# Latent-attention value products in unsplit float32, 64 columns wide, two query tiles in the two halves of TensorE's columns

## The chip, the cores and the metric

The kernel runs on one core of a Trainium2 chip. The metric is the device time of the whole program in microseconds (us). TensorE (PE) does matrix products into PSUM, VectorE (DVE), ScalarE (ACT) and GpSimd (POOL) do the elementwise work, and SyncE (SP) issues most transfers. "PEld" in a profile is PE's loading of the stationary operand.

## The reference

Two layers of an encoder with three kinds of attention side by side. The change is in the first kind, latent attention with 6 heads over 1,024 positions:

```python
kv = (rms_norm(c_kv, kv_lat_g) @ w_ukv).reshape(B, S, 6, 64 + 64)
k_nope, v_mla = kv[..., :64], kv[..., 64:]
...
s = jnp.einsum('bqhd,bkhd->bhqk', qi, k) * 96 ** -0.5     # qi: 128 queries
p = jax.nn.softmax(s, axis=-1)
o = jnp.einsum('bhqk,bkhe->bqhe', p, v)                   # v: 1,024 x 64 per head
```

The result, times a gate `silu(g_mla)`, goes to the output projection with those of the other two kinds.

## The kernel before

Each layer runs in stages: projections with the latent up-projection inside them (`kv_up`), differential attention (DiffItem, lines 720 to 790), neighbourhood attention (`na_item`, lines 1006 to 1048), latent attention (`mla_item`, from line 1161), output projection. Latent attention takes 48 items per layer: 6 heads times 8 query tiles of 128. Beside the items run, per head, the building of queries (`mla_q`) and keys (`mla_kn`, `mla_kt`), and towards the end the loading of the output weights (`load_wo`, casts at line 1229).

An item has three parts. `first`: six matmuls of scores into a PSUM tile S (lines 1172 to 1174; operands split into a high part in TensorE's rounded float32 form, fp32r, and a low remainder), a row maximum on DVE (L1177, L1178), the exponential on ACT (L1180), and normalising on POOL (L1182). `second`: eight PE transposes of the weights into two PSUM tiles T (L650); ACT copies each to the high part in SBUF (L138), then DVE subtracts to get the low part (L653). `third`, once per two query tiles (a pair): 16 matmuls (L1200) into the one PSUM tile O. There the stationary operand holds the value's high part in 64 columns and its low part in the other 64, and high and low weights of both query tiles (256 columns) stream through, so O's two halves are added at the end:

```python
for hl in range(2):
    PE.matmul(box["o"], mla[f"v{e}"][:, k], mla["PT"][b][:, hl, k], start=..., stop=...)
...
copy_act(u[m:m + 64], O[o:o + 64])
V.tensor_tensor(u[m:m + 64], O[m:m + 64], u[m:m + 64], ALU.add)
```

and POOL multiplies the sum into the gate (L1209). `kv_up`, 8 position tiles per layer, makes each head's values in the split form, with ACT for the high and DVE (L550) for the low part, and SP stores them in DRAM (`v_d`), from where POOL's queue fetches one head at a time (L1110).

The order of instructions on each engine is set when the program is built; each engine then runs its own list in order. PE's list is a mixture of the parts of neighbouring items. The tiles O have one buffer, S and T two each.

Of the kernel before, what the change touches and what calls it, by code (L numbers as in the profile page):

```python
# [12 lines left out]
F32 = mybir.dt.float32  # L13
F32R = mybir.dt.float32r
AF = mybir.ActivationFunctionType
ALU = mybir.AluOpType
# [11 lines left out]
    T=2,  # L28
# [14 lines left out]
def hybrid_encoder_kernel(  # L43
# [42 lines left out]
    dp = ctx.enter_context(tc.tile_pool(name="dp", bufs=1, space=bass.MemoryType.DRAM))  # L86
    xmid = dp.tile([S, D], F32, name="xmid")
    nk_d = dp.tile([128, 8, 384], F32, name="nk_d")
    v_d = dp.tile([8, 128, 6, 128], F32, name="v_d")
    wq_d = dp.tile([128, 3072], F32, name="wq_d")  # L90
    rpb_rep = dp.tile([depth * NA_H, 15, 64, 127], F32, name="rpb_rep")

# [44 lines left out]
    def copy_act(o, i, scale=1.0):  # L137
        A.activation(o, i, AF.Copy, scale=scale)  # L138
# [286 lines left out]
    for l in range(depth):  # L425
# [85 lines left out]

        kv_w = T(bp, "n1k", [128, 3072], F32R)
        wkv = kv_w[:, 0:1536].rearrange("p (l a h n) -> p l a h n", l=2, a=2, h=6)
        vst = Ring([kv_w[:, 1536 + i * 768:2304 + i * 768].rearrange("p (j e n) -> p j e n", e=2, n=128) for i in range(2)])
        raw = rawtile([128, 768])
        nc.sync.dma_start(raw, w_ukv[l])
        raw = raw.rearrange("p (h a n) -> p a h n", h=6, a=2)
# [2 lines left out]
            V.tensor_scalar(wkv[:, 0, a], raw[:, a], gcol, None, ALU.mult)  # L522
            V.scalar_tensor_tensor(wkv[:, 1, a], raw[:, a], gcol, f(wkv[:, 0, a]), ALU.mult, ALU.subtract)
        lkv = T(bp, "n1v", [128, 2, 1024], F32R)
        nk_t = T(bp, "n1q", [128, 8, 384])
        st_k = T(cp, "st_k", [128, 8, 6])
        rs_k = T(cp, "rs_k", [128, 8, 6])

# [6 lines left out]
        def kv_up(tt):  # L535
            hi, lo = (lkv[:, i, tt * 128:(tt + 1) * 128] for i in range(2))
            ps = psS()
            for a in range(2):
                o = ps[:, a * 512:a * 512 + 384]
                w0, w1 = (wkv[:, i, a].rearrange("p h n -> p (h n)") for i in range(2))  # L540
                PE.matmul(o, hi, w0, start=True, stop=False)
                PE.matmul(o, hi, w1, start=False, stop=False)
                PE.matmul(o, lo, w0, start=False, stop=True)
            V.tensor_copy(nk_t[:, tt], ps[:, 0:384])
            sumsq(ps[:, 0:384], 384, [(0, 384, 64, st_k[:, tt])], True)
            v = vst()
            pv = ps[:, 512:896].rearrange("p (j e n) -> p j e n", e=2, n=64)
            for e in range(2):
                copy_act(v[:, :, e, e * 64:e * 64 + 64], pv[:, :, e])
                V.tensor_tensor(v[:, :, e, 64 - e * 64:128 - e * 64], pv[:, :, e], f(v[:, :, e, e * 64:e * 64 + 64]), ALU.subtract)  # L550
            nc.sync.dma_start(v_d[tt], f(v).rearrange("p j e n -> p (j e) n"))

        def k_norm():
            V.tensor_tensor(st_k, st_k, st_lat[:, 2].unsqueeze(2).to_broadcast([128, 8, 6]), ALU.add)
            rstd_newton(rs_k.rearrange("p a b -> p (a b)"), st_k.rearrange("p a b -> p (a b)"), 96, 48)
            nc.sync.dma_start(nk_d, nk_t)

        pt = latent_t(2)
        copy_act(lkv[:, 0], pt)
# [511 lines left out]
        def mla_setup():  # L1071

            w = T(bp, "nd", [128, 6144], F32R)
            wq = w[:, 0:3072].rearrange("p (k l h n) -> p k l h n", k=2, l=2, h=6)
            mla["wq"] = wq
            for kc in range(2):
                raw = T(cp, "t2", [128, 640])[:, 0:576]
                nc.sync.dma_start(raw, w_uq[l, kc * 128:(kc + 1) * 128])
                raw = raw.rearrange("p (h n) -> p h n", h=6)
                gcol = vT[l][:, 32 + kc:33 + kc]  # L1080
                hi, lo = wq[:, kc, 0], wq[:, kc, 1]
                for a, b, d in ((0, 96, 0), (80, 96, 96), (64, 80, 112)):
                    n = b - a
                    V.tensor_scalar(hi[:, :, d:d + n], raw[:, :, a:b], gcol, None, ALU.mult)
                    V.scalar_tensor_tensor(lo[:, :, d:d + n], raw[:, :, a:b], gcol, f(hi[:, :, d:d + n]), ALU.mult, ALU.subtract)
            mla["v0"], mla["v1"] = (w[:, 3072 + i * 1024:4096 + i * 1024].rearrange("p (t d) -> p t d", t=8) for i in range(2))
            t = T(bp, "n1q", [128, 3, 1024], F32R)
            mla["lat"] = [t[:, i] for i in range(3)] + [w[:, 5120:6144]]
            mla["free"] = [w[:, i * 1024:(i + 1) * 1024] for i in range(3)] + mla["lat"][3:4] + mla["lat"][0:3]
            mla["free_v"] = [w[:, 3072 + i * 1024:4096 + i * 1024] for i in range(2)]  # L1090
            for kc in range(2):
                hi, lo = mla["lat"][2 * kc:2 * kc + 2]
                (V.tensor_copy if OPT["mla"]["lat"] == "V" else copy_act)(hi, latq[:, kc])
                G.tensor_tensor(lo, latq[:, kc], f(hi), ALU.subtract)
# [66 lines left out]
        def mla_item(h, qt):  # L1161
            e, b = h % 2, (qt // 2) % 2
            qhi, qlo, khi, klo = (forms[:, i] for i in ((0, 1, 6, 7), (2, 3, 4, 5))[e])
            ts_ = slice(qt * 128, (qt + 1) * 128)
            qs = slice(qt % 2 * 128, (qt % 2 + 1) * 128)
            box = {}

            def first():
                ps = psS()
                for a in range(2):  # L1170
                    o, ks = ps[:, a * 512:(a + 1) * 512], slice(a * 512, (a + 1) * 512)
                    PE.matmul(o, qhi[:, ts_], khi[:, ks], start=True, stop=False)  # L1172
# [12 lines left out]
            def second():  # L1185
                if "PT" not in mla:
                    mla["PT"] = {}
                if b not in mla["PT"]:
                    mla["PT"][b] = T(bp, f"R1{b}", [128, 2, 8, 256], F32R)
                PT = mla["PT"][b]  # L1190
                for kh in range(2):
                    ks = slice(kh * 4, kh * 4 + 4)
                    transpose_split(lambda i: box["p"][:, (kh * 4 + i) * 128:(kh * 4 + i + 1) * 128],
                                    PT[:, 0, ks, qs], PT[:, 1, ks, qs], 4)

            def pv(k):
                if k == 0:
                    box["o"] = psO()[:, 0:256]
                for hl in range(2):
                    PE.matmul(box["o"], mla[f"v{e}"][:, k], mla["PT"][b][:, hl, k], start=(k == 0 and hl == 0), stop=(k == 7 and hl == 1))  # L1200

            def finish():
                O = box["o"]
                u = T(cp, "t2", [128, 640])[:, 0:256]
                m, o = (64, 0) if e else (0, 64)
                copy_act(u[m:m + 64], O[o:o + 64])
                V.tensor_tensor(u[m:m + 64], O[m:m + 64], u[m:m + 64], ALU.add)
                g = sg[m:m + 64, h // 2, (qt // 2) * 256:(qt // 2 + 1) * 256]
# [165 lines left out]
```

## Time and profile before

| what | us |
|---|---|
| runs of the kernel before: median (lowest to highest of 3) | 1851.77 (1850.18 to 1853.68) |
| the profiled execution's own time | 1856.72 |
| its span, first to last instruction | 1854.9 |
| PE busy in the span | 1720.4 (93%) |
| DVE busy | 1338.3 (72%) |
| ACT busy | 947.9 (51%) |
| POOL busy | 811.2 (44%) |

Busy time is the union of an engine's instructions. A PE instruction counts until its last result is written, while the next is already streaming, so what a matmul takes of PE in a row of matmuls is read from start to start, not from its duration. The mean granted TensorE clock is 0.979 of full speed. A row of windows further down has these columns: the stretch, its length, busy time and instructions of PE, PEld, DVE, ACT and POOL, the granted clock, the share of the DMA engines and GB/s.

### The profile page before, as it was taken

What the parts mean: (1) busy time and instruction counts of PE and PEld (TensorE: products, weight loads), DVE (VectorE), ACT (ScalarE), POOL (GpSimd) and SP (SyncE); (2) the same over time, 40 slices, a digit from 0 to 9 for tenths busy, and PEclk for the clock granted to TensorE, in tenths of its full rate; (3) what the DMA queues carried; (4) which work ended last, traced back from release to release, by engine and by line L of the source; (5) the groups of instructions that cost most, each with busy time, mean ns of one, the idle gap of its engine ahead of it and who ended that gap; (6) DMA issues with size and microseconds to landing.
All of it is one profiled execution on the core that took longest, in us unless ns stands there. A gap on an engine that the chain in (4) does not pass through costs nothing. (4 is left out here: it accounts for less than half of the span.)

```text
span 1854.9 us, 28846 instructions
## 1 busy us (share of the span) xinstructions
PE 1720.4 (93%) x10724; PEld 1471.2 (79%) x10724; DVE 1338.3 (72%) x2634; ACT 947.9 (51%) x1954; POOL 811.2 (44%) x756
## 2 busy tenths in 40 slices
PE   4998889989899999989998988899999999999998
PEld 3978667778798888978878877777889888898877
DVE  6879877765975679995576487778565656999742
ACT  6522577771057667753342227777512765776500
POOL 4422435533345545473225043555415564556532
PEclk9999899999999999999999989999999999999999
DMA  9356000104323101131232520001221140003022
GB/s 285 100 131 168 13 24 23 35 1 123 104 55 54 59 1 24 35 89 33 80 127 59 109 82 23 24 12 35 66 86 29 21 102 1 12 24 81 23 91 91
DMA packets 141036, 117.60 MB, mean 63 GB/s; under 512 B 39834, under 2 KB 126048, under 8 KB 140384
## 3 DMA queue, kind: packets, MB, share of 16 engines
q1 hardware_dynamic: 116716, 103.61, 19.1%
q0 software_dynamic: 12480, 6.29, 2.0%
q10 hardware_dynamic: 11700, 5.85, 1.7%
q8 instruction: 85, 1.39, 0.3%
q14 instruction: 55, 0.45, 0.1%
HBM read 97.91 MB, written 23.68 MB: 66 GB/s over the span
## 5 line engine op out<-in xcount | busy, mean ns | idle before, releaser
L138 ACT ACTIVATE R<-T 128x512 fp32r<-128x512 f32 (+1 forms) x336 | 180.8, 550 | 125.5 <-PE T L638 61.8
L620 PE MATMUL F<-R,Pb 128*128 128x512 f32 x766 | 233.8, 420 | 11.7 <-ACT sg L138 11.7
L620 PEld LDWEIGHTS F<-R,Pb 128*128 128x128 f32 x766 | 141.5, 197 | 48.3 <-ACT sg L138 18.6
L1182 POOL TENSOR_SCALAR Pb<-Pb,sm 128x1024 f32<-128x1024 f32 x96 | 110.4, 1151 | 138.3 <-DVE sm L1178 69.3
L731 DVE TENSOR_REDUCE sm<-S 128x1 f32<-128x1024 f32 x128 | 153.2, 1218 | 16.0 <-PE S L726 14.5
L653 DVE TENSOR_TENSOR R<-T,R 128x512 fp32r<-128x512 f32 x192 | 129.1, 681 | 21.0 <-ACT R L138 20.1
L1180 ACT ACTIVATE Pb<-S,sm,rs_q 128x1024 f32<-128x1024 f32 x96 | 115.6, 1204 | 30.1 <-DVE sm L1178 26.4
L1200 PE MATMUL O<-R,nd 128*128 128x256 f32 x768 | 118.3, 292 | 6.3 <-DVE R L653 6.2
L1042 PE MATMUL O<-R,n1v 128*64 128x128 f32 x864 | 120.0, 280 | 1.2 <-ACT R L138 1.2
L1177 DVE TENSOR_REDUCE sm<-S 128x1 f32<-128x1024 f32 x96 | 116.5, 1213 | 5.4 <-PE S L1174 5.2
L650 PE MATMUL T<-ident,Pb 128*128 128x128 f32 x768 | 112.1, 275 | 6.8 <-DVE R L653 6.8
L1024 POOL TENSOR_SCALAR Pb<-Pb,sm 128x512 f32<-128x512 f32 (+1 forms) x96 | 74.5, 780 | 93.2 <-DVE sm L1023 87.7
L1200 PEld LDWEIGHTS O<-R,nd 128*128 128x128 f32 x768 | 102.9, 191 | 13.3 <-DVE R L653 9.1
L1042 PEld LDWEIGHTS O<-R,n1v 128*64 128x64 f32 x864 | 91.1, 136 | 21.7 <-issue 11.1
L1306 POOL TENSOR_TENSOR raw<-sg,raw 128x512 fp32r<-128x512 f32 x32 | 50.0, 1562 | 120.4 <-DVE raw L1305 120.3
L650 PEld LDWEIGHTS T<-ident,Pb 128*128 128x128 f32 x768 | 89.8, 142 | 16.1 <-DVE R L653 5.0
L801 POOL TENSOR_TENSOR Pb<-raw,Pb 128x512 fp32r<-128x512 f32 x32 | 43.8, 1372 | 125.2 <-DVE Pb L800 87.9
L733 ACT ACTIVATE nd<-S,sm 128x1024 f32<-128x1024 f32 x64 | 71.4, 1116 | 47.9 <-DVE sm L731 47.0
L457 ACT ACTIVATE t<-T 128x512 f32<-128x512 f32 x32 | 19.2, 599 | 141.9 <-DVE n1k L933 73.3
L737 POOL TENSOR_SCALAR nd<-nd,sm 128x1024 f32<-128x1024 f32 x48 | 58.7, 1223 | 65.0 <-DVE sm L735 64.8
L733 ACT ACTIVATE sg<-S,sm 128x1024 f32<-128x1024 f32 x64 | 71.3, 1115 | 27.7 <-DVE sm L731 14.1
L1172 PE MATMUL S<-R 128*128 128x512 f32 x192 | 84.8, 443 | 0.3
(439 smaller groups left out, 5247.4 us busy)
## 6 DMA issues: line engine op xcount, KB each, us to landing
raw<-in_w_in_dram SPq DMA_DIRECT2D x32, 512.0 KB
t<-in_ada_w_dram SPq DMA_DIRECT2D x40, 256.0 KB
n1k<-in_w_out_dram SPq DMA_DIRECT2D x16, 512.0 KB
v_d<-n1k SPq DMA_DIRECT2D x16, 384.0 KB
nl<-in_ada_w_dram SPq DMA_DIRECT2D x24, 256.0 KB
nd<-v_d POOLq DMA_DIRECT2D x12, 512.0 KB, 4.9
rpb_rep<-in_na_rpb_dram ACTq DMA_DIRECT2D x12, 476.2 KB
R<-in_ada_w_dram SPq DMA_DIRECT2D x8, 512.0 KB
```

The costliest lines, as they stand in the source:

```text
L138: A.activation(o, i, AF.Copy, scale=scale)
L620: ins = fn()
L650: PE.transpose(pt[:, i * 128:(i + 1) * 128], src_cols(i), ident)
L653: V.tensor_tensor(lo4, pv, f(hi4), ALU.subtract)
L731: V.tensor_reduce(stt[:, m:m + 1], ps, AX.X, ALU.max, negate=True)
L733: A.activation(p, ps.rearrange("p (k n) -> p k n", k=8), AF.Exp, bias=stt[:, m:m + 1], accum_out=stt[:, 2 + m:3 + m])
L1042: PE.matmul(O[m:m + 64, qs], nv[:, c0 + i, h * 64:(h + 1) * 64], PTf[qb][:, i, qs], start=(i == 0), stop=(i == n - 1), skip_group_check=True)
L1172: PE.matmul(o, qhi[:, ts_], khi[:, ks], start=True, stop=False)
L1177: V.tensor_reduce(stt[:, 0:1], ps, AX.X, ALU.max, negate=True)
L1180: A.activation(p, ps, AF.Exp, bias=stt[:, 3:4], scale=rs, accum_out=stt[:, 1:2])
L1182: mla["g"] = G.tensor_scalar(p, p, stt[:, 2:3], 0.0, ALU.mult, ALU.add)
L1200: PE.matmul(box["o"], mla[f"v{e}"][:, k], mla["PT"][b][:, hl, k], start=(k == 0 and hl == 0), stop=(k == 7 and hl == 1))
```

## The change

The values are stored and fetched unsplit, 64 columns per head. The weights are copied from PSUM unsplit, the first T tile of an item by ACT and the second by DVE. Each value product is a float32 matmul with a stationary operand of 64 columns: query tile 0 of the pair into partitions 0 to 63 of O, tile 1 into partitions 64 to 127, alternating. The end is one DVE multiplication per query tile of O with the gate; ACT's copy, DVE's addition and POOL's multiplication are gone.

```diff
-    v_d = dp.tile([8, 128, 6, 128], F32, name="v_d")
+    v_d = dp.tile([8, 128, 6, 64], F32, name="v_d")
...
-            V.tensor_copy(nk_t[:, tt], ps[:, 0:384])
+            kv = kvs()
+            V.tensor_copy(kv[:, 0:384], ps[:, 0:384])
+            copy_act(kv[:, 384:768], ps[:, 512:896])
             sumsq(ps[:, 0:384], 384, [(0, 384, 64, st_k[:, tt])], True)
-            v = vst()
-            pv = ps[:, 512:896].rearrange("p (j e n) -> p j e n", e=2, n=64)
-            for e in range(2):
-                copy_act(v[:, :, e, e * 64:e * 64 + 64], pv[:, :, e])
-                V.tensor_tensor(v[:, :, e, 64 - e * 64:128 - e * 64], pv[:, :, e], f(v[:, :, e, e * 64:e * 64 + 64]), ALU.subtract)
-            nc.sync.dma_start(v_d[tt], f(v).rearrange("p j e n -> p (j e) n"))
+            nc.sync.dma_start(nk_d[:, tt], kv[:, 0:384])
+            nc.sync.dma_start(v_d[tt], kv[:, 384:768].rearrange("p (h n) -> p h n", n=64))
...
-            nc.sync.dma_start(nk_d, nk_t)
...
                 for kh in range(2):
-                    ks = slice(kh * 4, kh * 4 + 4)
-                    transpose_split(lambda i: box["p"][:, (kh * 4 + i) * 128:(kh * 4 + i + 1) * 128],
-                                    PT[:, 0, ks, qs], PT[:, 1, ks, qs], 4)
+                    transpose_plain(lambda i: box["p"][:, (kh * 4 + i) * 128:(kh * 4 + i + 1) * 128],
+                                    mla["PT"][b][:, kh * 4:kh * 4 + 4, qs], 4, kh == 0)
 
             def pv(k):
+
                 if k == 0:
-                    box["o"] = psO()[:, 0:256]
-                for hl in range(2):
-                    PE.matmul(box["o"], mla[f"v{e}"][:, k], mla["PT"][b][:, hl, k], start=(k == 0 and hl == 0), stop=(k == 7 and hl == 1))
+                    box["o"] = psO()[:, 0:128]
+                for t in range(2):
+                    PE.matmul(box["o"][t * 64:t * 64 + 64], mla[f"v{e}"][:, k], mla["PT"][b][:, k, t * 128:(t + 1) * 128],
+                              start=(k == 0), stop=(k == 7), skip_group_check=True)
 
             def finish():
-                O = box["o"]
-                u = T(cp, "t2", [128, 640])[:, 0:256]
-                m, o = (64, 0) if e else (0, 64)
-                copy_act(u[m:m + 64], O[o:o + 64])
-                V.tensor_tensor(u[m:m + 64], O[m:m + 64], u[m:m + 64], ALU.add)
-                g = sg[m:m + 64, h // 2, (qt // 2) * 256:(qt // 2 + 1) * 256]
-                (V if h == MLA_H - 1 and qt == 7 else G).tensor_tensor(g, g, u[m:m + 64], ALU.mult)
+                m = 64 * e
+                for t in range(2):
+                    g = sg[m:m + 64, h // 2, (qt - 1 + t) * 128:(qt + t) * 128]
+                    V.tensor_tensor(g, g, box["o"][t * 64:t * 64 + 64], ALU.mult)
```

PE's list in the middle of a latent stage, before: L1172 to L1174 are scores, L650 transposes of weights, L1156 transposes of a key, L1200 the value products, which stand in two pieces of 9 and 7.

```order
L1174 MATMUL S_14641<-R_1460_12735 128x512
L1200 MATMUL O_14592<-R_1726_14400,nd_14027 128x256 x9
L650 MATMUL T_14627<-ident_75,Pb_12844 128x128 x4
L1156 MATMUL F_14735<-ident_75,n1k_14054 128x128 x4
L1200 MATMUL O_14592<-R_1726_14400,nd_14027 128x256 x7
L650 MATMUL T_14634<-ident_75,Pb_12844 128x128 x4
L1172 MATMUL S_14689<-R_1460_12735 128x512
```

The same place in the changed program (the line numbers are shifted: L634 transposes of weights, L1168 to L1170 scores, L1116 and L1117 a query, L1195 the value products):

```order
L634 MATMUL T_6984<-ident_75,Pb_4657 128x128 x4
L1195 MATMUL O_6996<-R_740_6073,nd_5840 64x128
L634 MATMUL T_6990<-ident_75,Pb_4657 128x128 x4
...
L1170 MATMUL S_7040<-R_489_4520 128x512
L1195 MATMUL O_6996<-R_740_6073,nd_5840 64x128 x8
L634 MATMUL T_7028<-ident_75,Pb_4657 128x128 x4
L1116 MATMUL F_7176<-n1q_5857,nd_5840 128x512
L1117 MATMUL F_7176<-n1q_5857,nd_5840 128x512
L1195 MATMUL O_6996<-R_740_6073,nd_5840 64x128 x7
L634 MATMUL T_7034<-ident_75,Pb_4657 128x128 x4
```

The 16 products of a pair now stand in pieces of 1, 8 and 7, between other matmuls that use all 128 columns. So it is in 42 of the 48 pairs of the program; in the other 6 the pieces are 1 and 15. That makes 138 pieces, where there were 114 before.

DVE's list around the end of a pair, before: L653 is the low part of the weights, L1207 the addition of O's halves, the rest belongs to the softmax and the queries.

```order
L653 TENSOR_TENSOR R_740_6090<-T_7401,R_740_6090 128x4x128
L1207 TENSOR_TENSOR t_911_7384<-O_7367,t_911_7384 64x256
L653 TENSOR_TENSOR R_740_6090<-T_7408,R_740_6090 128x4x128
L1177 TENSOR_REDUCE sm_7470<-S_7463 128x1
L1181 RECIPROCAL sm_7422<-sm_7422 128x1
L1178 TENSOR_TENSOR sm_7470<-sm_7470,rs_q_5886 128x1
```

And in the changed program: L639 is the copy of an item's second T tile, L1202 the multiplication with the gate.

```order
L639 COPY R_740_6073<-T_7331 128x4x128
L1173 TENSOR_REDUCE sm_7388<-S_7381 128x1
L1177 RECIPROCAL sm_7363<-sm_7363 128x1
L1174 TENSOR_TENSOR sm_7388<-sm_7388,rs_q_5869 128x1
L1202 TENSOR_TENSOR sg_1652<-sg_1652,O_7337 64x128 x2
L639 COPY R_758_6207<-T_7375 128x4x128
```

One copy per item stands where two subtractions stood, and the end of a pair is two small multiplications in the place of one addition.

## Rows read from the trace of the kernel before

**Rows 1.** Windows: busy us (instructions) of each engine in stretches of both latent stages.

```profile
668.00:795.00 127.00, 126.47 (x847) 113.38 (x847) 119.31 (x250) 93.09 (x180) 64.17 (x66) 1.00 0.11 26
795.00:850.00 55.00, 47.86 (x305) 41.08 (x303) 52.74 (x89) 34.00 (x63) 36.87 (x29) 0.97 0.23 66
...
1568.00:1697.00 129.00, 127.95 (x857) 114.64 (x856) 121.31 (x252) 94.30 (x182) 64.20 (x66) 1.00 0.11 26
1697.00:1750.00 53.00, 46.11 (x282) 39.77 (x282) 49.43 (x81) 30.83 (x57) 35.50 (x26) 0.94 0.21 60
```

**Rows 2.** Groups of PE from 795 to 850: count | busy, mean ns | idle before.

```profile
L1200 PE MATMUL O<-R,nd 128*128 128x256 f32 x111 | 17.2, 291 | 3.2 <-DVE R L653 3.1
L650 PE MATMUL T<-ident,Pb 128*128 128x128 f32 x108 | 16.3, 279 | 2.8 <-DVE R L653 2.8
L1172 PE MATMUL S<-R 128*128 128x512 f32 x24 | 11.1, 461 | 0.1
```

**Rows 3.** Timeline of PE in a latent stage: start, length, instruction, merged when alike.

```profile
673.83 0.39 PE L1174 MATMUL S<-R 128*128 128x512 f32 x1
674.06 1.24 PE L1200 MATMUL O<-R,nd 128*128 128x256 f32 x9
675.13 0.60 PE L650 MATMUL T<-ident,Pb 128*128 128x128 f32 x4
675.57 0.27 PE L1156 MATMUL F<-ident,n1k 128*128 128x128 f32 x1
```

**Rows 4.** A neighbourhood value product between transposes (timeline of PE), and its group.

```profile
574.57 0.60 PE L982 MATMUL F<-ident,n1q 128*128 128x128 f32 x4
575.10 0.43 PE L1042 MATMUL O<-R,n1v 128*64 128x128 f32 x2
575.46 0.66 PE L638 MATMUL T<-ident,Pb 128*128 128x128 f32 x4
...
L1042 PE MATMUL O<-R,n1v 128*64 128x128 f32 x864 | 120.0, 280 | 1.2 <-ACT R L138 1.2
```

**Rows 5.** Timeline of PE, differential value products: first and last of 32 records.

```profile
248.63 0.32 PE L764 MATMUL O<-nl,nd 128*64 128x128 f32 x1
248.63 0.32 PE L764 MATMUL O<-t,nd 128*64 128x128 f32 x1
248.79 0.27 PE L764 MATMUL O<-nl,nd 128*64 128x128 f32 x1
248.90 0.27 PE L764 MATMUL O<-nl,nd 128*64 128x128 f32 x1
...
250.31 0.27 PE L764 MATMUL O<-nl,nd 128*64 128x128 f32 x1
...
250.53 0.73 PE L620 MATMUL F<-R,Pb 128*128 128x512 f32 x2
```

**Rows 6.** Groups by form on DVE and ACT, whole span.

```profile
L653 DVE TENSOR_TENSOR R<-T,R 128x512 fp32r<-128x512 f32 x192 | 129.1, 681 | 21.0 <-ACT R L138 20.1
L138 ACT ACTIVATE R<-T 128x512 fp32r<-128x512 f32 x192 | 111.7, 597 | 62.5 <-PE T L650 60.3
L1207 DVE TENSOR_TENSOR t<-O,t 64x256 f32<-64x256 f32 x48 | 20.1, 420 | 13.5 <-ACT t L138 13.0
L1048 DVE TENSOR_TENSOR sg<-sg,O 64x512 f32<-64x512 f32 x24 | 16.4, 685 | 19.8 <-PE O L1042 19.5
L475 DVE COPY nd<-T 128x512 f32<-128x512 f32 x16 | 11.0, 686 | 11.1 <-PE T L448 11.0
L550 DVE TENSOR_TENSOR n1k<-S,n1k 128x192 fp32r<-128x192 f32 x32 | 10.8, 351 | 1.0
```

**Rows 7.** Timeline of DVE behind the last `kv_up`, layer 0 and layer 1.

```profile
157.24 0.76 DVE L800 CAST Pb<-raw 128x512 fp32r<-128x512 f32 x2 [0.48 <-DMA raw<-in_w_in_dram]
169.30 4.08 DVE L598 TENSOR_TENSOR nd<-nd,rs_d 128x1024 f32<-128x1024 f32 x2
...
1068.13 0.56 DVE L544 COPY n1q<-S 128x384 f32<-128x384 f32 x1 [1.00 <-PE S L543]
```

More of the change, by code (lines that the diff above doesn't have):

```diff
@@ L510, in rope_apply @@
             eng.tensor_tensor(dst[..., 16:32], t1[..., 16:32], t2[..., 0:16], ALU.add)
-        kv_w = T(bp, "n1k", [128, 3072], F32R)
-        wkv = kv_w[:, 0:1536].rearrange("p (l a h n) -> p l a h n", l=2, a=2, h=6)
-        vst = Ring([kv_w[:, 1536 + i * 768:2304 + i * 768].rearrange("p (j e n) -> p j e n", e=2, n=128) for i in range(2)])
+        wkv = T(bp, "n1k", [128, 1536], F32R).rearrange("p (l a h n) -> p l a h n", l=2, a=2, h=6)
         raw = rawtile([128, 768])
@@ L524, in hybrid_encoder_kernel @@
         lkv = T(bp, "n1v", [128, 2, 1024], F32R)
-        nk_t = T(bp, "n1q", [128, 8, 384])
+        kvs = T(bp, "n1q", [128, 4, 768])
+        kvs = Ring([kvs[:, i] for i in range(4)])
         st_k = T(cp, "st_k", [128, 8, 6])
@@ L1085, in mla_setup @@
                     V.scalar_tensor_tensor(lo[:, :, d:d + n], raw[:, :, a:b], gcol, f(hi[:, :, d:d + n]), ALU.mult, ALU.subtract)
-            mla["v0"], mla["v1"] = (w[:, 3072 + i * 1024:4096 + i * 1024].rearrange("p (t d) -> p t d", t=8) for i in range(2))
+            mla["v0"], mla["v1"] = (f(w[:, 3072 + i * 1024:3584 + i * 1024]).rearrange("p (t d) -> p t d", t=8) for i in range(2))
             t = T(bp, "n1q", [128, 3, 1024], F32R)
@@ L1188, in second @@
                 if b not in mla["PT"]:
-                    mla["PT"][b] = T(bp, f"R1{b}", [128, 2, 8, 256], F32R)
-                PT = mla["PT"][b]
+                    mla["PT"][b] = T(bp, f"R1{b}", [128, 8, 256])
                 for kh in range(2):
-                    ks = slice(kh * 4, kh * 4 + 4)
-                    transpose_split(lambda i: box["p"][:, (kh * 4 + i) * 128:(kh * 4 + i + 1) * 128],
-                                    PT[:, 0, ks, qs], PT[:, 1, ks, qs], 4)
+                    transpose_plain(lambda i: box["p"][:, (kh * 4 + i) * 128:(kh * 4 + i + 1) * 128],
+                                    mla["PT"][b][:, kh * 4:kh * 4 + 4, qs], 4, kh == 0)
             def pv(k):
                 if k == 0:
-                    box["o"] = psO()[:, 0:256]
-                for hl in range(2):
-                    PE.matmul(box["o"], mla[f"v{e}"][:, k], mla["PT"][b][:, hl, k], start=(k == 0 and hl == 0), stop=(k == 7 and hl == 1))
+                    box["o"] = psO()[:, 0:128]
+                for t in range(2):
+                    PE.matmul(box["o"][t * 64:t * 64 + 64], mla[f"v{e}"][:, k], mla["PT"][b][:, k, t * 128:(t + 1) * 128],
+                              start=(k == 0), stop=(k == 7), skip_group_check=True)
             def finish():
-                O = box["o"]
-                u = T(cp, "t2", [128, 640])[:, 0:256]
-                m, o = (64, 0) if e else (0, 64)
-                copy_act(u[m:m + 64], O[o:o + 64])
-                V.tensor_tensor(u[m:m + 64], O[m:m + 64], u[m:m + 64], ALU.add)
-                g = sg[m:m + 64, h // 2, (qt // 2) * 256:(qt // 2 + 1) * 256]
-                (V if h == MLA_H - 1 and qt == 7 else G).tensor_tensor(g, g, u[m:m + 64], ALU.mult)
+                m = 64 * e
+                for t in range(2):
+                    g = sg[m:m + 64, h // 2, (qt - 1 + t) * 128:(qt + t) * 128]
+                    V.tensor_tensor(g, g, box["o"][t * 64:t * 64 + 64], ALU.mult)
             return first, second, ([partial(pv, k) for k in range(8)] + [finish] if qt % 2 else [])
```

## The prediction

> **What bounds the kernel now.** The change lies in the two latent stages, so I read first the windows of those stages [rows 1]. For most of a stage (668 to 795 us, and 1568 to 1697) PE is busy 126.47 of 127 and 127.95 of 129 us at full clock: no pause in it, PE sets the pace. DVE is close behind (119.31 of 127). In the last 55 us, where the output weights are prepared on DVE and POOL beside the items, it is different: PE has 305 matmuls in 55 us, DVE is busy 52.74 of 55, and PE's pauses end on DVE's L653, the low part of the weights [rows 1, 2].
>
> How much PE waits there needs what a matmul takes from start to start. In the timeline nine value products take 674.06 to 675.13, 0.119 us each; four transposes 675.13 to 675.57, 0.11 each; a score matmul 0.23 [rows 3]. At those spacings the stretch holds 111 x 0.119 = 13.2 us of value products, 108 x 0.109 = 11.8 of transposes, 72 x 0.23 = 16.6 of scores (three groups like the one shown) and some 2 us of others [rows 2]: 43.6 of 55 us, so 11.4 are waiting, half clock included. Scaled by its 282 against 305 instructions, layer 1's stretch has 40.3 of 53, so 12.7 waiting [rows 1]. Together 24.1 us can at most be won from DVE in the latent stages; elsewhere in them PE time is end time, us for us.
>
> **The change, part by part.**
>
> *PE, the products themselves.* Before, a pair is 16 x 0.119 = 1.90 us. The new shape, 64 stationary columns and 128 streaming ones in float32, exists already: in neighbourhood attention, where one product is recorded as two matmuls (the two at 575.10 are one product [rows 4]), and in differential attention, where two query tiles go to the two halves alternately. There the second half's record starts 0.01 us or less behind the first, and the next pair of records 0.11 us later [rows 5]: both halves for the time of one, 0.22 us per product and half. The first record of such a run takes longer, which is priced below. In the list the 16 products of a pair stand as 1, 8 and 7, so one step alone and then four and four of two halves (1 and 15 give the same nine): 9 x 0.218 = 1.96 us. That is +0.06 a pair, +2.9 for 48.
>
> *PE, entering and leaving.* This is the large term. Take the product between transposes [rows 4]. Four transposes should take 0.44 us until the next matmul [rows 3]; from 574.57 to 575.10 it is 0.53: +0.09. The two records should take 0.22; from 575.10 to 575.46 it is 0.36: +0.14. The four transposes after it last 0.66 instead of 0.60 [rows 3, 4]: +0.06. So each visit to 64-column products costs 0.29 us, and PE shows no releaser for it. The long run of differential attention has the same marks: 0.16 instead of 0.11 at its start, 0.22 instead of 0.11 at its end [rows 5]. The old products used all 128 columns and changed nothing: their neighbours follow at plain spacing [rows 3]. The changed list makes 138 visits: 138 x 0.29 = +40.0 us.
>
> The trace prices the visit; the Trainium skill has a rule on it. TensorEngine Tiling (Array Packing), Key Properties, says that changing the tiling mode, not merely the tile, drains TensorE. It gives no price. By its Theoretical Speedup alone (up to twofold for 64 columns or fewer) the visits would be free and only the +2.9 above would remain; the rows agree with both sentences, and the measured 0.29 decides.
>
> PE's sum is +42.9 us, 0.89 a pair. Where it falls: the two waiting stretches hold 111/16 = 6.9 and about 6.4 pairs [rows 1, 2], 13.3; the other 34.7 lie where PE never pauses: +30.9 us, all on the path.
>
> *DVE, ACT and POOL in the latent stages.* DVE loses 192 subtractions of 0.681 (129.1 us) and 48 additions of 0.420, and gains 96 copies at the 0.686 of L475 (65.9) and 96 multiplications of 64x128 from PSUM. For those: 64x512 takes 685 ns and 64x256 420 [rows 6], so 128 columns come to some 0.29 by the same slope (bounds: nothing, and 0.42). Net 129.1 + 20.1 - 65.9 - 27.8 = 55.5 us less. In the waiting stretch that is 28 x 0.68 - 14 x 0.686 - 14 x 0.29 + 7 x 0.42, about 8 us, so DVE falls from 52.7 to some 45 of 55 and PE's new work there, 43.6 + 6.2 = 50, is the larger. ACT drops half its 192 copies and POOL its multiplication; both have room already (93.09 and 64.17 of 127 [rows 1]), worth nothing. A T tile is also free earlier: one reader of 0.6 to 0.7 us instead of two in turn.
>
> How much of the 24.1 comes back is not shown by any row. Bounds: none (the softmax chain through DVE and POOL waits as before) and all. DVE leaves the bound by a clear 5 us a stretch, so I take nearly all, with 5 us left: -19.1. The stretches together: +11.8 - 19.1 = -7.3.
>
> *`kv_up`.* DVE loses 32 subtractions of 0.351 [rows 6]. Only those behind DVE's last pause count. In layer 0 that pause is before 157.24, and DVE runs on through the norms at 169.30 with six of them in between (2.1 us); in layer 1 it is before 1068.13, with four (1.4) [rows 7]. I take -3, bounds 0 and -11. SP stores keys and values per tile, 16 transfers a layer instead of 9, each behind one copy instead of copy and subtraction; the weight loads queued behind them wait no longer than before. The buffers come round after four tiles. Half as many value bytes, off the path: nothing.
>
> Sum: +30.9 - 7.3 - 3 = **+21 us**. The profiled execution took 1856.7, 0.27% over the median 1851.8; against it the same sum gives 1878, against the median **1873**.
>
> **Rivals.** A measurement here tells 0.2% (3.7 us) from no change.
>
> *Faster: the visits cost nothing here.* What speaks for it: the rows of 0.29 come from other stages, and two neighbouring visits might merge. Then 2.9 - 19.1 - 3 = -19, so 1833. The point from which it decides: 138p + 2.9 - 19.1 - 3 = 0, p = 0.14 us a visit. Against it: single products, runs and both kinds of neighbour show the loss, and the neighbours here are the same transposes and wide matmuls. Chance 0.08. The Trainium skill's Theoretical Speedup would point this way if it stood alone.
>
> *The waits stay.* The pauses in the last stretch are passed on from softmax, POOL and the weight preparation rather than from L653; or a new wait comes in: O has one buffer, and the first single product of the next pair must wait for DVE's two multiplications, which stand in DVE's list behind reductions of 1.2 us, with the copy of a T tile queued behind them in turn. Between the pieces of 7 and the next 1 PE has only some 3 us of other work. Nothing recovered: +30.9 + 11.8 - 3 = +40, so 1892. Chance 0.2.
>
> *All waits go, and `kv_up` is worth double:* 42.9 - 24.1 - 6 = +13, 1865. Chance 0.13.
>
> *The halves don't overlap in broken runs:* 16 steps instead of 9, 7 x 0.218 x 48 = +73 on top, about 1946. Against it the clean alternation of [rows 5]. Chance 0.04.
>
> **How the numbers follow.** The main case has 0.55 (1867 to 1880). With the two cases beside it, and the visit's price off by 0.03 (4 us), the range is 1860 to 1894; free visits and lost overlap, 0.12, are left out, with some tail. Slower: main, waits stay, all waits go, no overlap, less a little that lands near zero: 0.89. Same: 0.03. Faster: 0.08.
>
> **What would show it.** Right: the new products in the latent stage spaced 0.11 per pair of records, halves within 0.01; about 0.29 lost around every piece; the stretch without pauses some 14 us longer for the same items; the last stretch 2 to 5 us shorter, with PE's waits on DVE mostly gone; DVE's busy time down by 55 to 66 us without a gain. Wrong: pieces that cost under 0.14; PE pausing before the single product until the L1202 multiplications; DVE still over 90% busy in the last stretch.

## The result, and the profile after

The changed kernel takes **1865.62 us** (median; 1864.99 to 1867.65) against 1852.51 for the kernel before on the same chip: ratio **1.0075** (95% interval 1.006 to 1.009), slower by 13 us. Forecast: 1873, range 1860 to 1894, slower with 0.89. The profiled execution took 1865.69 us, its span is 1863.9.

From the page of the kernel after: busy time by engine, and three groups with their idle time.

```profile
PE 1740.7 (93%) x11492; PEld 1453.5 (78%) x11492; DVE 1262.3 (68%) x2552; ACT 878.8 (47%) x1794; POOL 777.2 (42%) x710
...
L634 PE MATMUL T<-ident,Pb 128*128 128x128 f32 x1200 | 196.7, 284 | 5.0 <-DVE R L639 5.0
...
L1195 PE MATMUL O<-R,nd 128*64 128x128 f32 x1536 | 124.2, 280 | 0.9 <-DVE sg L1202 0.9
...
L639 DVE COPY R<-T 128x512 f32<-128x512 f32 x96 | 66.1, 689 | 30.8 <-PE T L634 28.7
```

DVE gave up 76 us and PE took 20 more. The wait has turned round: before, PE waited for DVE's L653, and that for ACT's copy [rows 2, 6]; now DVE's L639 waits 28.7 us for PE's transposes. (1,536 records of L1195 are 768 products: each is recorded twice, as in [rows 4].)

Windows of the latent stages, columns as in [rows 1]:

```profile
669.00:795.00 126.00, 126.00 (x997) 101.20 (x995) 92.36 (x214) 64.91 (x121) 50.08 (x48) 1.00 0.06 16
795.00:863.00 68.00, 63.55 (x510) 49.18 (x509) 52.03 (x103) 31.10 (x55) 36.74 (x27) 1.00 0.19 57
1568.00:1697.00 129.00, 129.00 (x1024) 103.34 (x1023) 94.66 (x219) 65.97 (x123) 50.96 (x49) 1.00 0.05 15
1697.00:1760.00 63.00, 59.17 (x474) 45.81 (x473) 49.07 (x96) 28.62 (x51) 35.86 (x26) 1.00 0.17 55
```

In the long stretches DVE is busy 92 of 126 us where it was 119 of 127; PE has no pause at all. In the last stretches the clock no longer falls (1.00, where it was 0.97 and 0.94), and DVE has room, 52 of 68.

The price of a visit, in PE's timeline:

```profile
701.67 0.40 PE L1170 MATMUL S<-R 128*128 128x512 f32 x1
702.00 1.09 PE L1195 MATMUL O<-R,nd 128*64 128x128 f32 x16
703.03 0.66 PE L634 MATMUL T<-ident,Pb 128*128 128x128 f32 x4
...
707.22 0.63 PE L634 MATMUL T<-ident,Pb 128*128 128x128 f32 x4
707.78 0.43 PE L1195 MATMUL O<-R,nd 128*64 128x128 f32 x2
708.15 0.66 PE L634 MATMUL T<-ident,Pb 128*128 128x128 f32 x4
708.56 0.48 PE L1168 MATMUL S<-R 128*128 128x512 f32 x1
```

A score matmul takes 0.23 us to the next start; here the piece begins 0.33 behind it (+0.10). Its 16 records are four steps of both halves, 4 x 0.218 = 0.87, but the transposes begin 1.03 behind (+0.16). The lone product at 707.78 begins 0.56 behind four transposes that need 0.44 (+0.12) and lasts 0.37 instead of 0.22 (+0.15). The remaining few hundredths are in the transposes behind, 0.66 us long instead of the plain 0.60 [rows 3].

Groups in the last stretch, 795 to 863 us, beside [rows 2]:

```profile
L1195 PE MATMUL O<-R,nd 128*64 128x128 f32 x256 | 20.9, 280 | 0.8 <-DVE sg L1202 0.8
L634 PE MATMUL T<-ident,Pb 128*128 128x128 f32 x126 | 20.0, 283 | 2.5 <-DVE R L639 2.5
...
L639 DVE COPY R<-T 128x512 f32<-128x512 f32 x16 | 11.0, 688 | 2.4 <-PE T L634 2.0
...
L1202 DVE TENSOR_TENSOR sg<-sg,O 64x128 f32<-64x128 f32 x16 | 4.6, 284 | 4.1 <-PE O L1195 3.9
```

The gate multiplications take 284 ns (estimated 0.29 us). PE's pauses on DVE are 0.8 and 2.5 us where they were 3.1 and 2.8; the 0.8 us is a wait for O's single buffer, which L1202 holds. In both latent stages together PE still pauses for 8.3 us, 2.4 of them for a score tile that ACT's exponential holds.

### The profile page after: what moved, and what is told of

The parts are those of the page before. It is cut to its first block, busy times and chain, and to the rows that moved or that the text cites. A ratio compares the mean times of both kernels' runs of the same rounds, so it can differ in the third digit from the quotient of the medians.

```text
span 1863.9 us, 29976 instructions
## 1 busy us (share of the span) xinstructions
PE 1740.7 (93%) x11492; PEld 1453.5 (78%) x11492; DVE 1262.3 (68%) x2552; ACT 878.8 (47%) x1794; POOL 777.2 (42%) x710
## 3 DMA queue, kind: packets, MB, share of 16 engines
q1 hardware_dynamic: 118732, 100.46, 18.4%
## 4 chain that ended last, share of the span: by engine, by line
PE 69%; DVE 17%; ACT 6%; DMA 4%; issue 2%; POOL 1%; SPq 1%; ACTq 0%; DVEq 0%; POOLq 0%
PE T L634 8%; PE O L1038 6%; PE F L616 5%; PE O L1195 5%; PE S L1307 3%; PE S L1306 3%; PE S L1305 3%; PE T L446 3%; PE T L447 3%; PE T L448 3%; DVE sm L727 3%; PE O L760 2%; PE S L1168 2%; PE S L1170 2%; PE S L1169 2%; DVE acc L274 2%
## 5 line engine op out<-in xcount | busy, mean ns | idle before, releaser
L616 PE MATMUL F<-R,Pb 128*128 128x512 f32 x766 | 230.1, 415 | 11.8 <-ACT sg L138 11.8
L138 ACT ACTIVATE R<-T 128x512 f32<-128x512 f32 x240 | 126.1, 530 | 162.1 <-PE T L634 160.9
L634 PE MATMUL T<-ident,Pb 128*128 128x128 f32 x1200 | 196.7, 284 | 5.0 <-DVE R L639 5.0
L1178 POOL TENSOR_SCALAR Pb<-Pb,sm 128x1024 f32<-128x1024 f32 x96 | 110.9, 1156 | 184.7 <-DVE sm L1177 174.8
L634 PEld LDWEIGHTS T<-ident,Pb 128*128 128x128 f32 x1200 | 133.4, 141 | 51.5 <-issue 31.9
L1176 ACT ACTIVATE Pb<-S,sm,rs_q 128x1024 f32<-128x1024 f32 x96 | 115.7, 1205 | 72.1 <-DVE sg L1202 20.7
L1195 PE MATMUL O<-R,nd 128*64 128x128 f32 x1536 | 124.2, 280 | 0.9 <-DVE sg L1202 0.9
L1195 PEld LDWEIGHTS O<-R,nd 128*64 128x64 f32 x1536 | 90.9, 136 | 30.7 <-issue 23.4
L1038 PEld LDWEIGHTS O<-R,n1v 128*64 128x64 f32 x864 | 91.1, 136 | 21.7 <-issue 11.1
L797 POOL TENSOR_TENSOR Pb<-raw,Pb 128x512 fp32r<-128x512 f32 x32 | 43.6, 1363 | 118.7 <-DVE Pb L796 86.6
L457 ACT ACTIVATE t<-T 128x512 f32<-128x512 f32 x32 | 19.1, 598 | 147.2 <-DVE n1k L929 73.3
L639 DVE COPY R<-T 128x512 f32<-128x512 f32 x96 | 66.1, 689 | 30.8 <-PE T L634 28.7
L1168 PE MATMUL S<-R 128*128 128x512 f32 x192 | 83.4, 436 | 2.4 <-ACT Pb L1176 2.4
```

The source lines that it names most:

```text
L616: ins = fn()
L634: ins = PE.transpose(pt[:, i * 128:(i + 1) * 128], src_cols(i), ident)
L1038: PE.matmul(O[m:m + 64, qs], nv[:, c0 + i, h * 64:(h + 1) * 64], PTf[qb][:, i, qs], start=(i == 0), stop=(i == n - 1), skip_group_check=True)
L1195: PE.matmul(box["o"][t * 64:t * 64 + 64], mla[f"v{e}"][:, k], mla["PT"][b][:, k, t * 128:(t + 1) * 128], start=(k == 0), stop=(k == 7), sk ...
```

## Experiments

All times are medians, with the ratio to the kernel before in the same session. The diffs show the main lines of each edit. The latent stages are taken apart in this table, both layers added, from the starts of PE's records between a stage's first score and its last value product. A *visit* is one uninterrupted piece of 64-column products, a *step* one product of each half (0.218 us). *Pieces*: value products, from the matmul ahead of a piece to the second one behind, less those neighbours at plain spacing and less PE's pauses (a stage's last piece to its last product). *Other*: all other matmuls at plain spacing (scores 0.227, transposes 0.109 and so on). *Rest*: what is left, PE's pauses, the cost of half clock (a granted clock of 0.5) outside the pieces and a floor of small gaps. (Of the 14.3 of the kernel after, 8.3 are pauses.)

| kernel | visits | stages | pieces | other | rest | time | ratio |
|---|---|---|---|---|---|---|---|
| before (first profile) | 0 | 455.1 | 96.9 | 326.7 | 31.5 | | 1 |
| copies_only | 0 | 434.8 | 92.5 | 323.1 | 19.2 | 1832.48 | 0.9905 |
| after | 138 | 473.7 | 137.7 | 321.7 | 14.3 | 1865.62 | 1.0075 |
| two_pieces | 96 | 454.3 | 112.4 | 323.1 | 18.8 | 1848.97 | 0.9988 |
| one_piece | 50 | 458.3 | 99.3 | 325.8 | 33.2 | 1853.14 | 1.0017 |
| four_tiles | 26 | 452.4 | 92.0 | 326.7 | 33.7 | 1847.25 | 0.9975 |
| wide | 94, full width | 508.3 | 167.3 | 322.6 | 18.4 | 1901.31 | 1.0268 |
| same_half | 128 | 545.2 | 208.3 | 324.4 | 12.5 | 1940.88 | 1.0482 |
| two_pieces_dve | 94 | 451.2 | 112.8 | 323.1 | 15.3 | 1846.89 | 0.9970 |
| one_piece_dve | 50 | 454.6 | 100.1 | 325.8 | 28.7 | 1851.90 | 0.9997 |
| four_tiles_dve | 26 | 450.3 | 90.2 | 326.7 | 33.4 | 1843.73 | 0.9960 |
| four_tiles_spread | 26 | 465.3 | 91.8 | 326.7 | 46.8 | 1858.50 | 1.0031 |

### Are the visits the price? Fewer of them

Theory: each visit costs about 0.29 us of PE, so fewer visits give time. Rival: the visits are free or hidden, and the loss is elsewhere. *one_piece* runs each pair's products together, second half of the keys first; *two_pieces* only swaps the order of the two tiles, by which the list falls into two pieces a pair:

```diff
-                if k == 0:
+                if k == 4:
-                for t in range(2):
+                for t in (1, 0):
-                              start=(k == 0), stop=(k == 7), ...
+                              start=(k == 4), stop=(k == 3), ...
-            ... [partial(pv, k) for k in range(8)] + [finish] ...
+            ... [partial(pv, k) for k in (4, 5, 6, 7, 0, 1, 2, 3)] + [finish] ...
```

(Of these lines two_pieces has the one with `for t`.)

> The changed kernel with the 16 value products of a pair in one piece (tile 1 first, blocks 4 to 7 before 0 to 3), so that PE's list has 50 visits to 64-column products instead of 138. Theory 'each visit costs about 0.29 us of PE': 88 visits fewer give -26, and 8 steps of both halves instead of 9 give 48 x 0.218 = -10; some of it is lost again where PE now waits for the last copy of the weights: 1830 to 1840. Rival 'visits are free, only the odd step counts': -10, about 1855. Rival 'the change is slower through new waits on DVE': within 5 us of 1866.

> The changed kernel with tile 1 ahead of tile 0 in each step, so that the pieces are 8 and 8: 96 visits, 8 steps. Visit theory: -42 x 0.29 = -12 and -10 for the odd step, 1840 to 1848, between the changed kernel and the one with one piece, about 13 us from the latter for 46 visits. Rival 'visits are free': 1855, the same as with one piece.

Measured: one_piece 1853.14 us (1.0017, interval 1.0008 to 1.0027), a miss: by its time alone it is where free visits would put it. two_pieces 1848.97 (0.9988, 0.9978 to 0.9998) is 1 us above its range, and 16 us below the kernel after by an order of two loops, which takes away 42 visits and the odd step; that it is faster than one_piece was not expected. On PE the theory held in both: over all pieces, each taken at the median of pieces of its length between the same neighbours, the kernel after spends 137.8 us, two_pieces 112.9, one_piece 99.3. With 9 steps a pair (after) or 8 (the others) at 0.218 that leaves 0.316, 0.304 and 0.312 us a visit. In one_piece the rest is 33 us where it is 19 in two_pieces, and took back more than the 46 visits fewer had given (see the waits below).

*four_tiles* computes value products once per four query tiles, 256 columns through each half:

```diff
-            e, b = h % 2, (qt // 2) % 2
+            e, b = h % 2, (qt // 4) % 2
-                    mla["PT"][b] = T(bp, f"R1{b}", [128, 8, 256])
+                    mla["PT"][b] = T(bp, f"R1{b}", [128, 8, 512])
-                    PE.matmul(box["o"][t * 64:t * 64 + 64], ..., mla["PT"][b][:, k, t * 128:(t + 1) * 128],
+                    PE.matmul(box["o"][t * 64:t * 64 + 64], ..., mla["PT"][b][:, k, t * 256:(t + 1) * 256],
```

> The changed kernel, with value products once per four query tiles: 256 columns stream through each half, in one piece of 8 steps, about 26 visits in all instead of 138 (50 in the one-piece version, which timed 1853 us). The products' own streaming time stays the same. If every visit costs PE some 0.3 us, the pieces cost PE 24 x 0.3 = 7 us less than in the one-piece version, about 92 us. Theory that the remaining loss of the one-piece version is PE waiting for its neighbours (softmax, copies, weight preparation): a longer piece gives the others more time at once but leaves less work between, so the time is between 1843 and 1853 us, with the pauses in the last stretch of each stage still there. Rival, that only visits count: 1846 us, below the two-piece version's 1849 us.

Measured: 1847.25 us (0.9975, 0.9966 to 0.9984). One piece in its PE timeline:

```profile
703.48 0.60 PE L634 MATMUL T<-ident,Pb 128*128 128x128 f32 x4
704.00 3.67 PE L1195 MATMUL O<-R,nd 128*64 128x256 f32 x32
707.61 1.09 PE L634 MATMUL T<-ident,Pb 128*128 128x128 f32 x8
708.46 0.48 PE L1168 MATMUL S<-R 128*128 128x512 f32 x1
```

32 records in 3.61 us: eight steps of 0.436 are 3.49, so a long run loses what a short one does: 0.08 at its entry (0.52 behind four transposes), 0.12 at its end, 0.06 in the first transposes behind it. All pieces cost 92.6 us (0.34 a visit), 7 less than in one_piece, as both expectations have it. The stages are 5.9 us shorter, the rest as large: what was gained is the visits. The time itself, 1847.25, does not tell the two expectations apart.

### Does it belong to the narrow columns?

*wide* keeps the unsplit float32 products, the copies and the gate, but its stationary operand is the values of two neighbouring heads, 128 columns, of which one head's result is used:

```diff
-                nc.gpsimd.dma_start(mla[f"v{h % 2}"], v_d[:, :, h]...)
+                nc.gpsimd.dma_start(mla[f"v{h % 2}"], v_d[:, :, min(h, 4):min(h, 4) + 2]...)
-                for t in range(2):
-                    PE.matmul(box["o"][t * 64:t * 64 + 64], mla[f"v{e}"][:, k], mla["PT"][b][:, k, t * 128:(t + 1) * 128], ...)
+                PE.matmul(box["o"], mla[f"v{e}"][:, k], mla["PT"][b][:, k], start=(k == 0), stop=(k == 7))
```

> The changed kernel with the values of two neighbouring heads as one stationary operand of 128 columns: still unsplit float32, the same copies and gate multiplications, pieces of 4 and 4 steps (94 visits), but all 128 columns are used, half of them for a head that is not read. A step is one product of 256 streaming columns, 0.436 us, so a pair takes 3.49 us instead of 1.96: 48 x 1.53 = 73 us more on PE than the two-piece version (96 visits, 1849 us), some 8 of it taken from the waits that are left there. Theory (the 0.29 us a visit belongs to the narrow columns): 94 x 0.29 = 27 us of that comes back, 1880 to 1898 us, and the neighbours of a piece follow at plain spacing. Rival (it belongs to the unsplit float32 product, whatever its width): 1908 to 1922 us, with the same 0.3 us lost around each piece.

Measured: 1901.31 us, between the two ranges, so the time alone does not tell. PE's timeline does:

```profile
701.27 0.40 PE L1170 MATMUL S<-R 128*128 128x512 f32 x1
701.50 1.89 PE L1194 MATMUL O<-R,nd 128*128 128x256 f32 x8
703.22 0.60 PE L634 MATMUL T<-ident,Pb 128*128 128x128 f32 x4
703.66 1.89 PE L1194 MATMUL O<-R,nd 128*128 128x256 f32 x8
705.39 0.60 PE L634 MATMUL T<-ident,Pb 128*128 128x128 f32 x4
```

The piece begins 0.23 behind the score, its eight records (four products) take 1.72, the transposes 0.44, the next piece 1.73: plain spacing everywhere. All 94 pieces cost 165.5 us, and 48 x 8 x 0.436 is 167.4: nothing is lost at a visit. So the 0.3 belongs to the 64 columns, and not to the 256 that stream here: four_tiles streams as many through 64 columns and pays. (My range was too low by two slips: two_pieces has 8 steps, not 9, so the products cost 84 us more instead of 73; and the rest gave back 0.4 instead of 8.) The Trainium skill, TensorEngine Tiling (Array Packing), Key Properties, says that a change of the tiling mode drains TensorE; the pair wide and two_pieces agrees, and shows the size it doesn't give.

### Do the halves overlap?

*same_half* sends both tiles to partitions 0 to 63 of O, into two column ranges. (The output is not the reference's; the number and shapes of the instructions are those of the kernel after.)

```diff
-                    PE.matmul(box["o"][t * 64:t * 64 + 64], ...
+                    PE.matmul(box["o"][0:64, t * 128:t * 128 + 128], ...
```

> The changed kernel, with both query tiles' value products sent to the same half of TensorE's columns, one after the other, into two column ranges of O. Visits, copies and everything else stay. Theory (two halves run in the time of one): each pair takes 16 steps of 0.218 us instead of 9, so 7 x 0.218 x 48 = 73 us more, 1925 to 1942 us; each pair of records starts 0.22 us behind the last. Rival (the halves do not overlap in broken runs): no change, about 1866 us.

Measured: 1940.88 us (1.0482, 1.0467 to 1.0497), 75 above the kernel after. In PE's timeline a piece of eight products:

```profile
696.35 1.96 PE L1195 MATMUL O<-R,nd 128*64 128x128 f32 x16
698.24 0.66 PE L634 MATMUL T<-ident,Pb 128*128 128x128 f32 x4
```

Sixteen records take 1.89 us to the next start; in the kernel after they took 1.03. The halves do run in the time of one, in short pieces too, and the visit price is the same here (0.308 us over 128).

### The copies alone, and `kv_up` alone

*copies_only* is the kernel before with the weights copied unsplit, the old products unchanged (the low part of the weights is left out, so the output is not the reference's):

```diff
-                    transpose_split(lambda i: box["p"]..., PT[:, 0, ks, qs], PT[:, 1, ks, qs], 4)
+                    transpose_plain(lambda i: box["p"]..., PT[:, ks, qs], 4, kh == 0)
```

> The kernel before with the weights copied unsplit (one copy per T tile, ACT and DVE in turn) and the low part left out of the products, which read the high part twice: same 16 products of 128 columns, no visits, DVE and ACT relieved. Theory 'DVE's relief gives back most of the 24 us that PE waits in the last stretches of the latent stages': 1830 to 1836. Rival 'those waits are passed on from softmax, POOL and weight preparation': 1848 to 1853.

Measured: 1832.48 us (0.9905, 0.989 to 0.992): -0.95%, 17.6 us, where the prediction had 19.1. The stages are 20.3 us shorter, 3.6 of them out-projection matmuls that now stand behind the stage.

*kv_only* is the kernel before with the new `kv_up` and its buffers; the old products take two heads' unsplit values (not the reference's output):

```diff
-            for e in range(2):
-                copy_act(v[:, :, e, e * 64:e * 64 + 64], pv[:, :, e])
-                V.tensor_tensor(v[:, :, e, 64 - e * 64:128 - e * 64], ..., ALU.subtract)
+            copy_act(kv[:, 384:768], ps[:, 512:896])
```

> The kernel before with only the up-projection's part of the change: values copied once by ACT, no subtraction on DVE, values and keys stored per tile; the products then read two heads' unsplit values in place of a value's high and low part, so that their shape and number stay. Theory 'only DVE's work behind its last pause counts': -3, about 1849. Rival 'the changed kernel's shorter time outside the latent stages, some 10 us in its profile, comes from this part': about 1842. Rival 'nothing': 1852.

Measured: 1846.87 us (0.9981, 0.9971 to 0.999): -3.5 us, where -3 was predicted. In layer 0 no gain is to be seen: the stretch up to the first differential value product is 222.6 us against 222.5, but profiles of the same instructions differ there by 4 us, so a small one may be hidden. The gain that shows lies at the start of layer 1's differential stage. A second profile of the kernel before was needed to read it:

> The kernel before, unchanged: a second profile of it. In its first profile the stretch from the last latent value product of layer 0 to the first differential value product of layer 1 is 257.2 us, in the profiles with the changed kv_up 246 to 252. Theory (that is kv_up and the pause before the half clock): again 255 to 259 us. Rival (the first profile was an unlucky one, its time is above all other runs): 248 to 252 us, and the whole span some 1849 us.

Measured: 1849.19 us, that stretch 251.6 us instead of 257.2, span 1847.4: the first profile was 7.5 us longer than this one, 5.6 of it here. As a reading of the 257.2 the theory fell. The difference is the granted clock. The windows of that stretch, first and second profile of the kernel before, then copies_only, which has the old `kv_up` too:

```profile
872.70:1129.90 257.20, 236.75 (x1183) 203.23 (x1181) 166.83 (x277) 84.23 (x233) 78.75 (x58) 0.95 0.30 86
869.40:1121.00 251.60, 230.95 (x1184) 198.65 (x1182) 166.61 (x277) 84.24 (x233) 79.14 (x58) 0.97 0.30 88
861.80:1119.00 257.20, 237.35 (x1192) 205.04 (x1192) 164.52 (x278) 84.37 (x234) 77.13 (x58) 0.95 0.29 86
```

PE is idle for 20.5, 20.7 and 19.9 us in them; it is busy for 6 us longer where the clock is lower. All three profiles with the old `kv_up` also have the same pause in this stretch. Kernel before, second profile:

```profile
1080.55 0.41 DVE L690 CAST n1k<-nd 128x512 fp32r<-128x512 f32 x1
...
1081.18 2.17 POOL L691 TENSOR_TENSOR n1k<-nd,n1k 128x512 fp32r<-128x512 f32 x1 [6.64 <-issue]
...
1082.34 2.10 DVE L507 TENSOR_TENSOR n1v<-nd,nl 128x1024 f32<-128x1024 f32 x1
...
1083.40 0.75 PE L701 MATMUL T<-identr,n1k 128*128 128x128 f32 x4 [4.06 <-POOL n1k L691]
```

PE's transposes wait 4.06 us for POOL's subtraction, that for DVE's cast at 1080.55, and that stood in DVE's list behind the norms. Then, in the window behind it, PE is busy throughout at a mean granted clock of 0.63:

```profile
1084.00:1090.00 6.00, 6.00 (x25) 4.79 (x23) 4.49 (x6) 1.20 (x2) 2.94 (x2) 0.63 0.01 3
```
In the kernel after, the same operations (L686, L687, L697) in the place where it waits longest for them:

```profile
1095.52 0.42 DVE L686 CAST n1k<-nd 128x512 fp32r<-128x512 f32 x1
...
1096.02 1.65 POOL L687 TENSOR_TENSOR n1k<-nd,n1k 128x512 fp32r<-128x512 f32 x1 [2.64 <-DVE n1k L686]
...
1097.72 0.53 PE L697 MATMUL T<-identr,n1k 128*128 128x128 f32 x4 [0.54 <-POOL n1k L687]
```

The wait is 0.54: 3.5 us shorter, as much as the measured gain. But DVE is not done sooner: from the first of its norms (L598, now L594) to the first of these transposes it is 14.7 us in both kernels. What changed is PE's list, which was mixed anew when the program was built: between `kv_up`'s last matmul and those transposes it has 173 matmuls of L446 to L448 where it had 131, some 5 us more to do meanwhile (kv_only, too, has 173).

### What do the versions with few visits wait for?

In one_piece PE stops for 5 us once in each stage. Its timeline before the first of these:

```profile
811.39 2.82 POOL L1223 TENSOR_TENSOR n1q<-n1k,nd 128x1024 fp32r<-128x1024 f32 x1 [0.63 <-DVE nw L1131]
...
811.97 2.26 DVE L1174 TENSOR_TENSOR sm<-sm,rs_q 128x1 f32<-128x1 f32 x1
...
816.01 2.34 POOL L1223 TENSOR_TENSOR n1q<-n1k,n1q 128x1024 fp32r<-128x1024 f32 x1 [0.70 <-DVE nw L1136]
816.41 1.95 DVE L1137 TENSOR_TENSOR rs_q<-nw 128x4 f32<-128x4 f32 x1
...
818.39 0.69 DVE L639 COPY R<-T 128x512 f32<-128x512 f32 x1
...
819.14 1.12 PE L634 MATMUL T<-ident,Pb 128*128 128x128 f32 x4 [5.05 <-DVE R L639]
```

DVE operations on one and four columns take 2 us, and end together with POOL's subtraction of the output weights; the copy that PE waits for is queued behind them. Alone, such an operation takes 0.15. The Trainium skill, SBUF — State Buffer, Who interferes with whom, says that a VectorE instruction with two SBUF inputs contends with a GpSimd one that reads SBUF, for a shared port pair that is an exclusive lock; these rows agree. Theory: that is the wait. Rival: it is the softmax chain behind one long piece. The *_dve* kernels move seven of the eight subtractions per layer to DVE:

```diff
-    wo=dict(lead=13.0, step=1.4, dve=()),
+    wo=dict(lead=13.0, step=1.4, dve=(0, 1, 2, 3, 4, 5, 6)),
```

> The two-piece version (about 96 visits, 1849 us), with the low parts of the output weights (seven of eight blocks per layer) subtracted on DVE instead of POOL. Theory (the small DVE operations of the softmax chain take 2 to 3 us instead of 0.3 while POOL runs its two-input subtraction, and PE's pauses in the last stretch come from that): the small operations keep to 0.4 us there and some 4 to 8 us come back over both layers, 1841 to 1845 us. Rival (the pauses come from the length of the chain itself, or DVE has no room): 1847 to 1853 us, with DVE some 10 us busier.

> The one-piece version (50 visits, 1853 us; PE pauses about 5 us once in each latent stage behind a small DVE operation that took 2 us beside POOL's subtraction), with the same seven subtractions on DVE. Theory of the held DVE operations: the two 5 us pauses go, with the half clock behind them, 1836 to 1845 us, and it is below the two-piece version by about the 46 visits it saves (13 us) if nothing else waits. Rival (the pause is the one long piece itself, which holds the transposes behind it): the pauses stay, 1850 to 1856 us.

> The four-tile version (26 visits, 1847 us) with seven of eight low parts of the output weights subtracted on DVE instead of POOL. In the one- and two-piece versions that took 0.2 to 0.4%, so 1840 to 1845 us; if the pauses of this version come from S waiting for the exponential, which this does not touch, 1846 to 1849 us.

Measured: 0.9970 (0.9956 to 0.9983), 0.9997 (0.9987 to 1.0007) and 0.9960 (0.9945 to 0.9976), each 0.15 to 0.20% below its counterpart, about 3 us. Only for one_piece do the two intervals not overlap; for the others it is the agreement of the three that speaks. In time the first lies between its two ranges, the second in the rival's, the third in the theory's. From 795 to 863 us, L1174 in one_piece and then in one_piece_dve:

```profile
L1174 DVE TENSOR_TENSOR sm<-sm,rs_q 128x1 f32<-128x1 f32 x12 | 5.1, 425 | 0.1
```

```profile
L1174 DVE TENSOR_TENSOR sm<-sm,rs_q 128x1 f32<-128x1 f32 x14 | 2.1, 153 | 0.1
```

The small operations are freed, and the 5 us pauses are gone. But the waits of one_piece_dve from 1697 to 1760 us show what comes next:

```profile
PE S L1168 <- ACT Pb L1176: 4.1, 2, 3.1
PE O L1195 <- DVE R L639: 2.7, 2, 1.5
```

PE waits for a score tile that ACT's exponential still holds. So the held DVE operations were one link, worth some 3 us; the chain itself is the next.

*four_tiles_spread* begins the weight preparation earlier (lead 20, step 2.4). Its loads overwrite data of the last heads that is still to be read, so its output is not the reference's; the operations are the same.

> The four-tile version with the preparation of the output weights begun 20 items before the end of a stage instead of 13, 2.4 items apart instead of 1.4. Theory (what PE still waits for in the last stretch is the softmax chain held by that preparation): the same work in a longer stretch in which PE is the bound, some 10 of the 38 us that PE waits in both stages come back, 1835 to 1842 us. Rival (the buffers come free late anyway, or the pauses are the chain itself): 1845 to 1849 us.

Measured: 1858.50 us (1.0031, 1.0019 to 1.0043), slower than four_tiles; the rest of the stages grew from 33.7 to 46.8 us. The theory fell. That the preparation, spread out, disturbs more items would fit, and so would waits for the buffers that it takes early; the two were not tried apart.

The best version is four_tiles_dve, 1843.73 us, 0.4% below the kernel before and 1.1% below the change as made.

## Why the prediction was right, and where its sum was off

**Products and visits.** 138 visits at 0.29 were to cost 40.0 us; they cost 138 x 0.316 = 43.6. By the same medians the pieces of copies_only are 92.0 and those of the kernel after 137.8, so they cost 45.8; the sum had 42.9. The three rows of the neighbourhood stage [rows 4] gave the right price for another stage, and wide shows why it may be carried over: it belongs to the columns, not to the neighbours. So this step of the forecast is right, its price a little low.

**Recovered waits.** -19.1 predicted, -17.6 timed with the copies alone. L653 was the main wait. Its removal did not take all: 9.5 us of pauses are left in copies_only, most of them on the copy that took L653's place. DVE's busy time fell by 76 us instead of 55 to 66; a part of the surplus is the small L1178 (now L1174), on one column, which takes 28.0 us in all where it took 45.4.

**`kv_up`.** -3 predicted, -3.5 timed. The size came out, but by luck: in layer 0 no gain shows, and in layer 1 it is not DVE's share at its end but a PE pause of 4.06 us that became 0.54, because PE's list was mixed anew.

**The sum** is where a size was off: +21 predicted, +13.1 by the medians (+13.9 by the ratio, interval 11 to 17). The term that fails is PE's: taken as +42.9, all of it time ("+30.9" in the stretches without pauses and "+11.8" in the others). By the ratios 0.75% + 0.95% + 0.19% = 1.89% it is +35.0 us of time, for 45.8 of PE work. From copies_only to the kernel after the stages grow by 38.9: pieces +45.2, rest -4.9, other -1.4. So some 5 us of the new work took the place of time that PE still lost after the copies were cheap (19.2 us of rest, then 14.3): pauses went from 9.5 to 8.3, half clock from 1.7 to nothing, what is left of the 5 is small gaps. The prediction let 5 us of waits stand and charged the visits in full beside them. The last 4 us lie outside these stages. The stretch from layer 0's last latent value product to layer 1's first differential one is 257.2 us in copies_only and 246.4 in the kernel after (248.1 to 251.7 in all others with the new `kv_up`): 3.5 of that is `kv_up`, and most of what is left goes with the granted clock, 0.95 and 0.97, the same two values that the two profiles of the kernel before have there. So it may be chance of the profiles; how much of it belongs to the change is open.

**The stretches.** The prediction had the two last stretches shorter by 7.3 us. From the 36th score to the 48th they are 105.3 us before, 94.4 in copies_only and 105.5 after: the copies gave 10.9 there, the visits took 11.1, and the stretches did not get shorter. Of the other 9.4 us that copies_only gained, 3.6 are the matmuls moved behind the stage; some 6 came from stretches in which the windows of [rows 1] show PE busy nearly throughout, so busy time seems to hide short waits there. From the 9th score to the 36th, 27 pairs in both layers, the stages grew by 20.0 us (214.2 to 234.2), 0.74 a pair for 0.89 predicted; from copies_only (210.9) it is 0.86, which fits.

**The rivals.** Free visits: refuted by the piece costs of five kernels. Waits stay: refuted by copies_only; the pause on O's single buffer exists, 0.8 us in the last stretch. No overlap: refuted by same_half. "All waits go and `kv_up` is worth double" gave 1865, the measured time, by chance: the copies gave 17.6 us and not 24.1, 8.3 us of pauses remain, and `kv_up` gave 3.5 and not 6.

## What to carry to other kernels

On a TensorE-bound stretch, count how often the list enters and leaves matmuls of another column width, not only how many there are: at 0.3 us a visit, three pieces a pair cost 0.9 us, twice what the cheaper copies and `kv_up` gave here (21 us over 48 pairs). Run such products together, but look at what the longer piece makes wait: from 96 visits to 26 the time fell by 2 us where 70 x 0.3 = 21 were saved on PE, because PE no longer set the time. And cheap elementwise work won from a neighbour engine counts only until the next wait.

## What the hardware showed that was not expected

- Changing between 64 and 128 stationary columns costs 0.30 to 0.34 us per visit (five kernels, 26 to 138 visits), at full clock; at full width (wide) nothing.
- A two-input DVE operation stretches to the end of a POOL subtraction beside it: 2.26 us instead of 0.15 for one column in one_piece. In the second profile of the kernel before, L507 took 2.10 us beside POOL's L691, and 1.21 at 1078.29, before L691 began.
- Two profiles of the kernel before differ by 7.5 us of span, 5.6 of it in one stretch in which PE is idle for about 20.5 us each time and the granted clock is 0.95 in one and 0.97 in the other: a stretch's length is worth a second profile, and a look at the clock, before it is explained.
